# A two-layer decoder trunk: the down projection of 16 FFN slices as seven products per set, between gate and up chunks

## The chip, the cores and the metric

The kernel runs on one core of a Trainium2 chip. The metric is the device time in microseconds (us) of one execution. PE is TensorE, which multiplies matrices (PEld is its loading of the stationary operand); DVE is VectorE, ACT is ScalarE, POOL is GpSimd, SP issues most of the DMAs.

## The reference

Two layers on 512 tokens of width 1024. Layer 0 mixes tokens by sliding-window attention, layer 1 by a chunked spatial gating unit; each layer then has a SwiGLU FFN. Every mixer and every FFN stands between two RMS norms and adds to the residual:

```python
def swiglu(h, w_gate_up, w_down):
    gu = h @ w_gate_up                                        # 1024 -> 2 x 2816
    return (jax.nn.silu(gu[..., :D_FF]) * gu[..., D_FF:]) @ w_down   # 2816 -> 1024

for i in range(DEPTH):
    m = swa_sink_attention(rmsnorm(x, ...), ...) if i % 2 == 0 else chunked_sgu(rmsnorm(x, ...), ...)
    x = x + rmsnorm(m, norm_mix_post[i])
    x = x + rmsnorm(swiglu(rmsnorm(x, norm_ffn_pre[i]), w_gate_up[i], w_down[i]), norm_ffn_post[i])
```

Everything is float32. The 2816 hidden units of an FFN are 22 slices of 128.

## The kernel before, in words

**Numbers in two parts.** PE multiplies a float32 number as a high part in a rounded format and a low part, the rest. So every product is three matmuls (`mm3`): high by high, high by low, low by high. What PE reads has to be split first: ACT copies the high part (`wh`, L257), DVE subtracts it from the raw number for the low part (`wl`, L253).

**Weights as one stream.** All weights lie in device memory in the order of their use, in chunks of 8 blocks of 128 x 128 (512 KB). `fetch` has SP load a chunk into one of `NRAW` = 2 raw tiles; `split` makes it into a `wh` and a `wl` tile of a ring of `NW` = 17 tiles of 4 KB per partition, in which row vectors also lie for a while. `blk` gives PE a block and counts how often a chunk is still needed; a chunk that nobody needs is given back.

**Order of the work.** The order of the instructions of PE, DVE and ACT is written out by a planner in the kernel itself: it keeps a clock for PE (`now`) and one for each helper, and runs small generators (`Side`) when they are due. `split_idle` decides when the next chunk is split: never before the previous one has issued its low part; at once when its slack has sunk to a margin of the stage (`PLAN`, first number: 2.0 in stage 2, 8.0 in 3, 10.0 in 6, 6.0 in 7); otherwise only when the helpers are idle and no generator marked as a chain is due soon. The slack is the number of chunks ahead times `pace` less a constant:

```python
slack = max(now[0], hold[0]) + (c - cur[0] - 1) * pace[0] - max(now[0], busy["v"], busy["a"]) - 2.4
```

**The FFN** (`ffn`). PE computes gate and up of one slice (48 matmuls of 512 columns: 8 depth blocks, two outputs, three passes), ACT takes silu from PSUM (L614), DVE multiplies by up (L620), ACT and DVE split the result (L624, L627). The first three slices run in two halves of the tokens. After 11 slices their down projection follows: for each column half all four token tiles of 128 tokens at once (`tok_proj`), ACT copies the results to `m` (L678). After the other 11 slices comes the second half of the down projection, first column half for all tokens, then the second column half token by token; DVE adds the result to `m` (L689), and `Tok` runs the token's norm and residual (squares on ACT, the gain on DVE or POOL L509/L503, the reciprocal root on DVE, L522) while PE goes on with the next token. For the next layer the tokens are scaled, transposed by PE (L459) and split (L472, L476). In the last FFN the last token's second column half is computed in two parts of 256 columns (L711), and the rows are stored.

**Attention and the gating layer** use the same ring. Tiles of the tag `rt` (three of 2 x 512) hold pairs of high and low parts there; `p` tiles (two of 4 x 512) hold scores, later gating inputs.

Of the kernel before, what the change touches and what calls it, by code (L numbers as in the profile page):

```python
# [6 lines left out]
F32 = mybir.dt.float32  # L7
# [13 lines left out]
HJ = NJ // 2  # L21
# [4 lines left out]
NW = 17  # L26
# [5 lines left out]
NRAW = 2  # L32
# [16 lines left out]

V0 = 0  # L50
# [5 lines left out]
SV0 = GU0 + 3 * NJ * KT  # L56
# [5 lines left out]
NBLK = GU1 + 3 * NJ * KT  # L62

def uses(i):

    if i < Q0 or WO0 <= i < GU0 or SO0 <= i < GU1:
        return 4
    if SV0 <= i < SO0:  # L70
        return 4 if i < SU0 or SV1 <= i < SU1 else 2 if i < SV1 else 1
    if i < WO0:
        return 1
    b = i - GU0 if i < SV0 else i - GU1
    f, b = divmod(b, 3 * HJ * KT)
    if b >= 2 * HJ * KT:
        return 4
    return 2 if f == 0 and b < 3 * 2 * KT else 1
# [3 lines left out]
def trunk_kernel(ctx, tc, x_t, xt, w, cols, rows, ws_t, consts, out):  # L82
# [136 lines left out]
    left = [0] * NCH  # L219
    for i in range(NBLK):  # L220
        left[i // CB] += uses(i)

    def fetch(free=0.0, most=NBLK):
        while len(raws) < min(NCH, len(chunks) + NRAW, most):
            c = len(raws)
            if c == NLATE:
                load_x()
            if c == NLATE + 1:
                nc.sync.dma_start(c_msk[:, 0:256], consts[:, 1024:1280])
                nc.sync.dma_start(c_msk[:, 256:384], consts[:, 1408:1536])  # L230
                nc.sync.dma_start(cs[:], consts[:, 0:1024])
                busy["d"] += 2.5
            raw = rawp.tile([P, CB * P], F32, tag="raw", name=nm("raw"))
            nc.sync.dma_start(raw[:], w[c])
            busy["d"] = max(busy["d"], now[0], free) + 1.46
            raws[c] = (raw, busy["d"] + DLAT)

    def split():
        c = len(chunks)
        fetch()  # L240
        raw, ready = raws[c]
# [68 lines left out]
    def drop(n=1):  # L310
        used[0] -= n

# [296 lines left out]
    def ffn(base, nx_in, g1o, nx_out):  # L609
# [30 lines left out]

        h = hsrc(nx_in)

        def gu(g, b0, j, hf):
            grab("acc")
            grab("acc")
            ps = (acc(), acc())
            for k in range(KT):
                rh, rl = h(k, hf)
                for u in range(2):
                    wh, wl = blk(b0 + (j * KT + k) * 2 + u)  # L650
                    mm3(ps[u][:, hf], wh, wl, rh, rl, k == 0, k == KT - 1)
                tick()
            evac_gu(g, j, *ps, hf)

        m = None
        for f in range(2):
            stage[0] = (2 if base == GU0 else 6) + f
            b0 = base + f * (HJ * KT * 3)
            ga = [gp.tile([P, 8, S], F32R, tag="ga", name=nm("ga")) for _ in range(2)]
            gb = [gp.tile([P, 3, S], F32R, tag="gb", name=nm("gb")) for _ in range(2)]  # L660
            g = [[ga[i][:, k] if k < 8 else gb[i][:, k - 8] for k in range(HJ)] for i in range(2)] + [{}]
            j0 = 0
            if f == 0:
                pace[0] = 2.5
                for hf in halves:
                    for j in range(3):
                        gu(g, b0, j, hf)
                j0 = 3
            pace[0] = 5.1
            for j in range(j0, HJ):  # L670
                gu(g, b0, j, full)
            d0 = b0 + HJ * KT * 2
            l = gsrc(g)
            if f == 0:
                m = new_m()
                for c in range(2):
                    def evac0(t, ps):
                        nc.scalar.activation(m[t][c][:], ps[:], AF.Copy)  # L678
                        A(S, now[0] + 0.2)
                    tok_proj(d0 + c * HJ * 4, HJ, l, evac0)  # L680
                continue
# [10 lines left out]
            tok_proj(d0, HJ, l, lambda t, ps: add(t, 0, ps), False)  # L692
            hold[0] = now[0] + NB * HJ * 0.65
            for t in range(NB if nx_out is not None else NB - 1):
                grab("acc")
                ps = acc()
                for k in range(HJ):
                    tok_mm(ps, l, t, k, d0 + HJ * 4 + 4 * k, k == 0, k == HJ - 1)
                add(t, 1, ps)
            if nx_out is None:  # L700
                t = NB - 1
                until(lambda: toks[0].done)
                for i, hf in enumerate(halves):
                    grab("acc")
                    ps = acc()[:, 0:256]
                    for k in range(HJ):
                        lh, ll = l(k, slice(t * P, (t + 1) * P))
                        wh, wl = blk(d0 + HJ * 4 + 4 * k, 4 if i else 0, 4)
                        mm3(ps, lh, ll, wh[:, hf], wl[:, hf], k == 0, k == HJ - 1)
# [3 lines left out]
            drop()  # L713


    def attention(nx_in, g1o, nx_out):
# [263 lines left out]
        hold[0] = now[0] + NB * 8 * 0.65 + 10  # L980
        for t in range(NB):
            tok = Tok(t, m[t], g1, nx_out)
            for c in range(2):
# [7 lines left out]
        drop(2)  # L991


    def sgu(nx_in, g1o, nx_out):
# [157 lines left out]
        drop()  # L1152
# [73 lines left out]
def _layout(inputs):  # L1226
# [30 lines left out]
    def ffn(i):  # L1257
        gu = blocks(a["ffn_w_gate_up"][i]).reshape(KT, 2, NJ, P, P)
        dn = blocks(a["ffn_w_down"][i])
        for h in range(2):  # L1260
            js = slice(h * HJ, (h + 1) * HJ)
            seq.append(gu[:, :, js].transpose(2, 0, 1, 3, 4).reshape(-1, P, P))
            for c in range(2):
                seq.append(flat(dn[js][:, 4 * c:4 * c + 4]))
# [12 lines left out]
    assert w.shape[0] == NBLK  # L1277
    w = np.ascontiguousarray(w.reshape(NBLK // CB, CB, P, P).transpose(0, 2, 1, 3).reshape(NBLK // CB, P, CB * P))

# [40 lines left out]
```

## Time and profile before

| | |
|---|---|
| median of 3 runs | 1066.5 us (1066.02 to 1067.13) |
| the profiled execution | 1067.36 us, its span 1065.6 us |
| mean granted clock | 0.994 |
| PE, DVE, ACT busy | 1046.0, 524.8, 438.4 us |
| matmuls, weight splits | 5237 recorded, 176 |
| read from device memory | 102.13 MB |

The profile is of one execution. Busy time of PE counts matmuls that overlap in its pipeline, so it says little about how well PE is fed; the chain of work and the list of waits say more. The last pieces of the down projections end at about 365, 549, 874 and 1059 us.

### The profile page before, as it was taken

To read this page: it belongs to the slowest core of one execution; us is meant where nothing else is said; L and a number is where in the kernel's file an instruction comes from. 1 tells how busy PE (TensorE), PEld (TensorE's weight loads), DVE (VectorE), ACT (ScalarE), POOL (GpSimd) and SP (SyncE) were. 2 spreads that over 40 slices of the span, in tenths; PEclk is the share of its full clock that TensorE was granted. 3 is DMA by queue.
4 is the path that set the end of the run, shared out by engine and by line. 5 is a ranking of instruction groups with operands and counts; after the bars stand their busy time and mean duration, and the time that the engine had idled before them with its cause. 6 is when DMAs were issued, how large, how long until landed. Compare 5 with 4: busy or idle time off the path is not lost.

```text
span 1065.6 us, 13311 instructions
## 1 busy us (share of the span) xinstructions
PE 1046.0 (98%) x5237; PEld 869.6 (82%) x5237; DVE 524.8 (49%) x1074; ACT 438.4 (41%) x775; POOL 24.2 (2%) x22
## 2 busy tenths in 40 slices
PE   7998998999999999999999999999999999999997
PEld 6875666988888888888889888899888888888886
DVE  6699679743332233332474867584333223333335
ACT  4799676632322223222255444573223222232210
POOL 2000002000000000000000000100000000000000
PEclk9999999999999999999999999999999999999999
DMA  8322101433233322223133233034223332222302
GB/s 292 125 93 80 60 21 60 131 127 99 99 99 99 99 99 95 94 92 135 59 119 100 79 125 106 28 120 151 90 97 98 99 99 99 99 99 98 101 1 80
DMA packets 29839, 105.10 MB, mean 99 GB/s; under 512 B 3344, under 2 KB 3872, under 8 KB 29776
## 3 DMA queue, kind: packets, MB, share of 16 engines
q1 hardware_dynamic: 29088, 103.10, 29.1%
q8 instruction: 41, 0.67, 0.3%
q10 hardware_dynamic: 576, 0.92, 0.2%
q0 software_dynamic: 112, 0.23, 0.2%
q14 instruction: 22, 0.18, 0.0%
HBM read 102.13 MB, written 2.10 MB: 98 GB/s over the span
## 4 chain that ended last, share of the span: by engine, by line
PE 88%; DVE 7%; ACT 2%; DMA 1%; issue 1%; POOL 0%; DVEq 0%; ACTq 0%; POOLq 0%
PE acc L204 86%; DVE wl L253 1%; DVE p L828 1%; ACT rt L746 1%; PE aux L459 1%; DVE p L859 1%; DMA raw<-w 1%; PE acc L888 1%; DMA c_cols<-cols 1%; PE aux L896 0%; DVE rt L740 0%; ACT wh L257 0%; ACT p L850 0%; DVE hl L1168 0%; PE aux L457 0%
## 5 line engine op out<-in xcount | busy, mean ns | idle before, releaser
L253 DVE TENSOR_TENSOR wl<-raw,wh 128x1024 fp32r<-128x1024 f32 x174 | 214.5, 1234 | 413.0 <-PE acc L204 340.4
L204 PE MATMUL acc<-hh,wh 128*128 128x512 f32 (+1 forms) x960 | 352.1, 367 | 0.0
L204 PE MATMUL acc<-hl,wh 128*128 128x512 f32 (+1 forms) x960 | 349.8, 364 | 0.0
L204 PE MATMUL acc<-hh,wl 128*128 128x512 f32 (+1 forms) x960 | 349.7, 364 | 0.0
L257 ACT ACTIVATE wh<-raw 128x1024 fp32r<-128x1024 f32 x176 | 185.8, 1058 | 220.4 <-PE acc L204 184.6
L204 PE MATMUL acc<-wh,ga 128*128 128x512 f32 (+1 forms) x736 | 236.2, 392 | 2.7 <-DVE ga L915 2.7
L204 PEld LDWEIGHTS acc<-hh,wh 128*128 128x128 f32 x960 | 181.0, 188 | 29.1 <-issue 0.2
L204 PEld LDWEIGHTS acc<-hh,wl 128*128 128x128 f32 x960 | 180.9, 188 | 28.9
L204 PEld LDWEIGHTS acc<-hl,wh 128*128 128x128 f32 x960 | 181.0, 189 | 28.8 <-issue 0.2
L204 PEld LDWEIGHTS acc<-wh,ga 128*128 128x128 f32 x736 | 138.3, 189 | 35.1 <-issue 4.9
L204 PE MATMUL acc<-wl,ga 128*128 128x512 f32 (+1 forms) x368 | 142.3, 387 | 0.0
L614 ACT ACTIVATE t<-acc 128x512 f32<-128x512 f32 (+1 forms) x50 | 27.3, 545 | 146.5 <-PE acc L204 146.5
L204 PEld LDWEIGHTS acc<-wl,ga 128*128 128x128 f32 x368 | 69.8, 190 | 12.8
L204 PE MATMUL acc<-wh,gb 128*128 128x512 f32 (+1 forms) x198 | 61.9, 383 | 0.0
L624 ACT ACTIVATE ga<-t 128x512 fp32r<-128x512 f32 (+1 forms) x38 | 21.5, 565 | 53.5 <-DVE t L620 53.4
L204 PEld LDWEIGHTS acc<-wh,gb 128*128 128x128 f32 x198 | 36.9, 188 | 7.2
L503 POOL TENSOR_TENSOR m<-m,row 128x512 f32<-128x512 f32 x12 | 17.2, 1433 | 1020.6 <-ACT acc L381 1020.6
L204 PE MATMUL acc<-wh,hh 128*128 128x512 f32 (+1 forms) x96 | 34.4, 368 | 4.4 <-ACT wh L257 4.4
L204 PE MATMUL acc<-wl,gb 128*128 128x512 f32 (+1 forms) x99 | 37.9, 383 | 0.0
L381 ACT ACTIVATE acc<-m 128x512 f32<-128x512 f32 x30 | 18.0, 598 | 46.5 <-DVE m L689 42.1
L204 PE MATMUL acc<-wh,hl 128*128 128x512 f32 (+1 forms) x96 | 34.3, 367 | 0.7 <-DVE hl L1168 0.7
L627 DVE TENSOR_TENSOR ga<-t,ga 128x512 fp32r<-128x512 f32 (+1 forms) x38 | 23.1, 607 | 21.1 <-ACT ga L624 21.1
(124 smaller groups left out, 830.4 us busy)
## 6 DMA issues: line engine op xcount, KB each, us to landing
raw<-w SPq DMA_DIRECT2D x176, 512.0 KB, 3.5
row<-rows SPq DMA_DIRECT2D x8, 512.0 KB, 4.5
xg<-xt SPq DMA_DIRECT2D x4, 512.0 KB, 7.3
x<-x_t SPq DMA_DIRECT2D x4, 512.0 KB, 7.3
out<-x SPq DMA_DIRECT2D x4, 256.0 KB, 2.1
out<-x ACTq DMA_DIRECT2D x3, 256.0 KB, 2.1
cs<-consts SPq DMA_DIRECT2D x1, 512.0 KB, 7.2
t<-ws_t SPq DMA_DIRECT2D x2, 256.0 KB, 4.3
```

What stands on the lines that cost most here:

```text
L204: nc.tensor.matmul(ps, a, b, start=start, stop=stop)
L253: nc.vector.tensor_tensor(wl[:], raw[:], wh[:].bitcast(F32), ALU.subtract)
L257: nc.scalar.activation(wh[:], raw[:], AF.Copy)
L381: nc.scalar.activation(junk, src, AF.Square, accum_out=s[:, c:c + 1])
L459: nc.tensor.transpose(dst, self.src[t][k // 4][:, (k % 4) * P:(k % 4 + 1) * P], ident)
L503: nc.gpsimd.tensor_tensor(self.m[c][:], self.m[c][:], self.g1[:, cols2[c]], ALU.mult)
L614: nc.scalar.activation(t1[:, hf], pg[:, hf], AF.Silu)
L624: nc.scalar.activation(g[0][jj][:, hf], t1[:, hf], AF.Copy)
L627: nc.vector.tensor_tensor(g[1][jj][:, hf], t1[:, hf], g[0][jj][:, hf].bitcast(F32), ALU.subtract)
L746: nc.scalar.activation(ro[o:o + 32, hf], t1[q * 32:q * 32 + 32, hf], AF.Identity, bias=b[q * 32:q * 32 + 32])
L828: nc.vector.tensor_tensor_reduce(pt[:, 2 * g2 + g, i, 0:nk], sc[i][:, g * 256:g * 256 + nk], mask[:, 256 - nk:256], 0.125, sink_bc[:, pr * ...
L859: nc.vector.tensor_scalar(p(j), p(j), sm[:, j:j + 1], None, ALU.mult)
```

## The change

Of the 22 slices of an FFN the first 16 go through the down projection in two sets of eight (`SETS`). In a set the hidden units are taken in quads of four slices. Tokens are cut into two halves of 256, hidden units into two parities (even and odd slices of the quad), output columns into two halves of 512. The 2 x 2 by 2 x 2 block product is formed by seven block products instead of eight (`PRODUCTS`: which two blocks of the activations and which two of the weights are added or subtracted first; `TARGETS`: where each result is added or subtracted).

- The weights of a product with two blocks are loaded as two raw tiles, added on DVE and then split; `NRAW` is 4, `NW` is 15, `fetch` counts raw tiles.
- Slices 0 to 15 are kept unsplit after silu and product (`evac_raw`). A chain generator (`operands`) adds two blocks on DVE where needed and splits the sum into one of three `rt` tiles, up to three ahead of PE.
- `ITEMS` is the order of PE's work: items of a product and a quad (12 matmuls), alternating with items of half a slice of gate and up (24 matmuls). The first set's products run between slices 8 to 15, the second's between slices 16 to 21.
- `settle` adds a product's two PSUM banks to the rows of `m` (the first set's first contributions are copied by ACT).
- The last six slices run as before per token tile, but tokens 0 and 1 together, then token 2, then token 3, each with both column halves.
- The row tile of the gain is counted as free only after its tokens have used it (`drop_after`), in attention and gating too; gating gives its `rt` tiles back.
- The host lays the down weights out by quad, parity and column half.

```diff
-NW = 17
+NW = 15
...
-NRAW = 2
+NRAW = 4
+SETS = (8, 8)
+AJ = sum(SETS)
+BJ = NJ - AJ
+NQ = AJ // 4
...
+PRODUCTS = (
+    (((0, 0), (1, 1), 1), ((0, 0), (1, 1), 1)),
+    (((1, 0), (0, 0), -1), ((0, 0), (0, 1), 1)),
+    (((1, 1), None, 0), ((1, 0), (0, 0), -1)),
+    (((0, 1), (1, 1), -1), ((1, 0), (1, 1), 1)),
+    (((0, 0), None, 0), ((0, 1), (1, 1), -1)),
+    (((0, 0), (0, 1), 1), ((1, 1), None, 0)),
+    (((1, 0), (1, 1), 1), ((0, 0), None, 0)),
+)
+TARGETS = (
+    (("=", 0, 0), ("=", 1, 1)),
+    (("+", 1, 1),),
+    (("=", 1, 0), ("+", 0, 0)),
+    (("+", 0, 0),),
+    (("=", 0, 1), ("+", 1, 1)),
+    (("+", 0, 1), ("-", 0, 0)),
+    (("+", 1, 0), ("-", 1, 1)),
+)
...
+        ps = [("p", (n, p), q) for p in range(len(PRODUCTS)) for q in range(q0, q0 + SETS[n] // 4)]
+        gs = [("g", j, half) for j in range(j0, j1) for half in range(2)]
+        np_, ng = len(ps), len(gs)
+        while ps or gs:
+            out.append(gs.pop(0) if gs and len(gs) * np_ >= len(ps) * ng else ps.pop(0))
...
-        while len(raws) < min(NCH, len(chunks) + NRAW, most):
+        while len(raws) < min(NCH, most) and raw_used[0] + len(STREAM[len(raws)][0]) <= NRAW:
...
+            raw_used[0] -= 1
...
+        def high_low(f):
+            yield f
+            nc.scalar.activation(wh[:], raw[:], AF.Copy)
+            yield from low(A(CB * P, f))
+        if len(tiles) == 2:
+            op = ALU.add if STREAM[c][1] > 0 else ALU.subtract
+            nc.vector.tensor_tensor(raw[:], raw[:], tiles[1][:], op)
+            f = V(CB * P, ready)
+            raw_used[0] -= 1
+            fetch(f)
+            chunks[c] = [wh, wl, None, None, f]
+            chunks[c][2] = Side(high_low(f), f)
+            return
...
-        slack = max(now[0], hold[0]) + (c - cur[0] - 1) * pace[0] - max(now[0], busy["v"], busy["a"]) - 2.4
+        slack = max(now[0], hold[0]) + (c - cur[0] - 1) * pace[0] - max(now[0], busy["v"], busy["a"]) - (2.4 if len(STREAM[c][0]) == 1 else 3.7)
...
+    def drop_after(toks):
+        def side():
+            while any(len(t.half) < 2 for t in toks):
+                yield now[0] + 0.2
+            drop()
...
+        stage[0] = 2 if base == GU0 else 6
...
+        def operands():
+            for n, (p, q) in enumerate(todo):
+                while n >= spent[0] + len(ring):
+                    yield now[0] + 0.2
...
+                    yield from take("t")
+                    t = tmp()[:].rearrange("p (a t) -> p a t", a=2)
+                    nc.vector.tensor_tensor(t, src, view(y), ALU.add if sign > 0 else ALU.subtract)
+                    src = t
...
+                hi, lo = (r.rearrange("p (a t) -> p a t", a=2) for r in ring[n % len(ring)])
+                nc.scalar.activation(hi, src, AF.Copy)
+                f = A(S, f)
+                yield f
+                nc.vector.tensor_tensor(lo, src, hi.bitcast(F32), ALU.subtract)
+                made[p, q] = V(S, f), hi, lo
...
+        Side(operands(), now[0], True)
+        pace[0] = 4.0
...
+        def settle(p, ps):
+            for sign, th, c in TARGETS[p[1]]:
+                for i in range(2):
+                    d = m[2 * th + i][c][:]
+                    if sign == "=" and not p[0]:
+                        nc.scalar.activation(d, ps[i][:], AF.Copy)
                         A(S, now[0] + 0.2)
...
+                    else:
+                        nc.vector.tensor_tensor(d, d, ps[i][:], ALU.subtract if sign == "-" else ALU.add)
+                        V(S, now[0] + 0.2)
...
+                q0 = sum(SETS[:a[0]]) // 4
+                last = q0 + SETS[a[0]] // 4 - 1
+                if b == q0:
+                    banks = two()
+                until(lambda: (a, b) in made)
+                f, hi, lo = made[a, b]
+                wait(f)
+                for kp in range(2):
+                    for i in range(2):
+                        ts = slice(i * P, i * P + P)
+                        wh, wl = blk(at + 4 * kp, 4)
+                        mm3(banks[i][:], hi[:, kp, ts], lo[:, kp, ts], wh, wl,
+                            b == q0 and kp == 0, b == last and kp == 1)
+                        tick()
+                spent[0] += 1
+                if b == last:
+                    settle(a, banks)
+                    give("acc")
+                    give("acc")
+            at += CB
...
+        pace[0] = 5.1
+        stage[0] += 1
...
+            ends = [(0, 0), (0, 1), (1, 0), (1, 1)]
+            if nx_out is None:
+                ends.pop()
+            ends = [((0, 1), 0), ((0, 1), 1)] + [((2 + i,), c) for i, c in ends]
+            for n, (ts, c) in enumerate(ends):
+                if n == 2:
+                    hold[0] = now[0] + 4 * BJ * 0.65
+                for t in ts:
+                    grab("acc")
+                ps = [acc() for _ in ts]
+                for k in range(BJ):
+                    for t, q in zip(ts, ps):
+                        tok_mm(q, l, t, k, d0 + c * BJ * 4 + 4 * k, k == 0, k == BJ - 1)
+                for t, q in zip(ts, ps):
+                    add(t, c, q)
```

## Rows read from the trace of the kernel before

**Rows 1.** The clocks: the span in us from the first to the last instruction and the mean granted clock of TensorE.

```profile
core 0: 1065.6 us, clock 0.994
```

**Rows 2.** The page, part 1: busy time of each engine, its share of the span, its instructions.

```profile
PE 1046.0 (98%) x5237; PEld 869.6 (82%) x5237; DVE 524.8 (49%) x1074; ACT 438.4 (41%) x775; POOL 24.2 (2%) x22
```

**Rows 3.** The chain of work that ended last, in order of time, pieces merged: start, length in us, what it is. The two longest pieces.

```profile
205.46 336.82 PE acc L204 x1548
...
714.43 344.14 PE acc L204 x1617
```

**Rows 4.** The list of waits: who waited for whom, total us, times, longest. The first three from 205 to 1059 us, the last for PE alone from 175 us on.

```profile
DVE wl L253 <- PE acc L204: 340.4, 100, 4.6
ACT wh L257 <- PE acc L204: 184.6, 67, 4.4
...
ACT wh L257 <- DMA raw<-w: 28.0, 21, 4.1
...
PE acc L204 <- DVE ga L915: 2.7, 1, 2.7
```

**Rows 5.** The timeline of DVE, GpSimd and PE in two places of the attention stage: start, us, engine, line, operation, tiles, count, and in brackets the idle time before it and what ended it.

```profile
71.80 2.35 DVE L253 TENSOR_TENSOR wl<-raw,wh 128x1024 fp32r<-128x1024 f32 x2
...
171.19 1.62 POOL L503 TENSOR_TENSOR m<-m,row 128x512 f32<-128x512 f32 x1 [2.08 <-ACT acc L381]
171.59 2.29 DVE L253 TENSOR_TENSOR wl<-raw,wh 128x1024 fp32r<-128x1024 f32 x1
...
174.54 1.20 PE L204 MATMUL acc<-wh,ga 128*128 128x512 f32 x2 [2.67 <-DVE ga L915]
```

**Rows 6.** The timeline of PE: first and last of 28 consecutive matmuls of 512 columns in the second FFN, and first and last of 30 of 256 columns in the gating layer.

```profile
799.79 0.39 PE L204 MATMUL acc<-hl,wh 128*128 128x512 f32 x1
...
805.91 0.39 PE L204 MATMUL acc<-hl,wh 128*128 128x512 f32 x1
...
560.32 0.28 PE L204 MATMUL acc<-hh,wh 128*128 128x256 f32 x1
...
563.79 0.28 PE L204 MATMUL acc<-hh,wl 128*128 128x256 f32 x1
```

**Rows 7.** Groups by line from 205 to 1059 us, DVE and ACT: busy us, mean ns of one, then the idle time before them.

```profile
L253 DVE TENSOR_TENSOR wl<-raw,wh 128x1024 fp32r<-128x1024 f32 x148 | 181.8, 1229 | 411.9 <-PE acc L204 340.4 <-ACT wh L257 71.3
L620 DVE TENSOR_TENSOR t<-t,acc 128x512 f32<-128x512 f32 (+1 forms) x47 | 29.6, 629 | 0.0
L627 DVE TENSOR_TENSOR ga<-t,ga 128x512 fp32r<-128x512 f32 (+1 forms) x36 | 22.2, 618 | 21.1 <-ACT ga L624 21.1
L689 DVE TENSOR_TENSOR m<-acc,m 128x512 f32<-128x512 f32 x15 | 10.0, 688 | 24.3 <-PE acc L204 24.3
...
L257 ACT ACTIVATE wh<-raw 128x1024 fp32r<-128x1024 f32 x148 | 156.4, 1058 | 212.7 <-PE acc L204 184.6 <-DMA raw<-w 28.0
L614 ACT ACTIVATE t<-acc 128x512 f32<-128x512 f32 (+1 forms) x47 | 26.1, 556 | 145.8 <-PE acc L204 145.8
L624 ACT ACTIVATE ga<-t 128x512 fp32r<-128x512 f32 (+1 forms) x36 | 20.6, 573 | 53.5 <-DVE t L620 53.4
```

**Rows 8.** Stretches: from and to in us, length, then busy us and instructions of PE, PEld, DVE, ACT and POOL, the granted clock, the DMA share, GB/s.

```profile
15.00:20.00 5.00, 4.28 (x36) 4.08 (x35) 4.63 (x6) 2.29 (x5) 0.75 (x1) 1.00 1.01 390
25.00:30.00 5.00, 5.00 (x22) 3.79 (x21) 2.41 (x5) 0.77 (x2) 0.00 (x0) 1.00 0.28 98
120.00:125.00 5.00, 5.00 (x24) 3.04 (x22) 2.59 (x6) 1.59 (x4) 0.00 (x0) 1.00 0.89 313
165.00:170.00 5.00, 5.00 (x23) 2.64 (x23) 4.90 (x13) 3.96 (x10) 1.30 (x1) 1.00 0.26 74
170.00:175.00 5.00, 2.33 (x9) 1.65 (x9) 4.88 (x6) 2.44 (x7) 1.62 (x1) 0.96 0.11 39
175.00:180.00 5.00, 5.00 (x20) 4.07 (x20) 4.96 (x23) 1.67 (x3) 1.29 (x1) 0.70 0.29 99
205.00:317.00 112.00, 112.00 (x560) 95.53 (x559) 42.81 (x50) 37.67 (x50) 0.00 (x0) 1.00 0.33 106
```

**Rows 9.** What SP's queue waited for (total us, times, longest), and the weight loads among the DMA issues of the page (count, KB each, median us from issue to landing).

```profile
SPq L234 <- DVE wl L253: 823.7, 158, 30.8
...
raw<-w SPq DMA_DIRECT2D x176, 512.0 KB, 3.5
```

**Rows 10.** The timeline where the first FFN hands over to the gating layer: token 0's and token 1's last down halves (L689), the first transposes (L459), the first matmul of the next layer and the last low part of tokens 0 and 1 (L476).

```profile
525.32 0.69 DVE L689 TENSOR_TENSOR m<-acc,m 128x512 f32<-128x512 f32 x1 [2.81 <-PE acc L204]
528.69 1.41 DVE L522 SCALAR_TENSOR_TENSOR x<-m,rc,x 128x512 f32<-128x512 f32 x2
532.80 0.69 DVE L689 TENSOR_TENSOR m<-acc,m 128x512 f32<-128x512 f32 x1 [2.70 <-PE acc L204]
542.12 0.60 PE L459 MATMUL aux<-c_id,m 128*128 128x128 f32 x4
549.34 0.48 PE L204 MATMUL acc<-wh,hh 128*128 128x512 f32 x1
551.49 0.87 DVE L476 SCALAR_TENSOR_TENSOR hl<-aux,c_cols,hh 128x256 fp32r<-128x256 f32 x2
```

**Rows 11.** The end of the same chain as in rows 3: start, length in us, what it is.

```profile
1058.60 0.44 DVE m L711
...
1062.03 0.40 DVE x L567
```

More of the change, by code (lines that the diff above doesn't have):

```diff
@@ L20 @@
 NJ = FF // P
-HJ = NJ // 2
 EPS = 1e-6
@@ L61 @@
 GU1 = SO0 + 64
[L62 to L78, printed above, removed]
+NBLK = GU1 + FFB
 @with_exitstack
@@ L232, in fetch @@
                 busy["d"] += 2.5
[L233 to L236, printed above, removed]
+            tiles = []
+            for b in reversed(STREAM[c][0]):
+                raw = rawp.tile([P, CB * P], F32, tag="raw", name=nm("raw"))
+                nc.sync.dma_start(raw[:], w[b])
+                busy["d"] = max(busy["d"], now[0], free) + 1.46
+                tiles.insert(0, raw)
+            raw_used[0] += len(tiles)
+            raws[c] = (tiles, busy["d"] + DLAT)
     def split():
@@ L240, in split @@
         fetch()
-        raw, ready = raws[c]
+        tiles, ready = raws[c]
+        raw = tiles[0]
         assert used[0] + 2 <= NW
@@ L311, in drop @@
         used[0] -= n
+    def drop_after(toks):
[3 more added lines that the diff above has]
+            drop()
+        Side(side(), now[0])
     xs = [xp.tile([P, D], F32, tag=f"x{k}", name=f"x{k}") for k in range(NB)]
@@ L644, in gu, with two @@
+        h = hsrc(nx_in)
+        def gu(ps, b, js, hf):
+            for k in js:
+                rh, rl = h(k, hf)
+                for u in range(2):
+                    wh, wl = blk(b + 2 * k + u)
+                    mm3(ps[u][:, hf], wh, wl, rh, rl, k == 0, k == KT - 1)
+                tick()
+        def two():
             grab("acc")
             grab("acc")
[L646 to L678, printed above, removed]
-                        A(S, now[0] + 0.2)
-                    tok_proj(d0 + c * HJ * 4, HJ, l, evac0)
-                continue
+            return acc(), acc()
@@ new lines, in ffn, with quad @@
+        pa = [ptile() for _ in range(2)]
+        g8 = gp.tile([P, 8, S], F32, tag="ga", name=nm("ga"))
+        ga = gp.tile([P, 8, S], F32R, tag="ga", name=nm("ga"))
+        gb = [gp.tile([P, 3, S], F32R, tag="gb", name=nm("gb")) for _ in range(2)]
+        cells = [ga[:, k] for k in range(8)] + [gb[i][:, k] for i in range(2) for k in range(3)]
+        g = [cells[0:BJ], cells[BJ:2 * BJ], {}]
+        raw_ready = {}
+        def quad(q):
+            return pa[q] if q < 2 else g8[:, 4 * q - 8:4 * q - 4]
@@ new lines, in raw_g, with parity, pair_tile @@
+        def raw_g(j):
+            return quad(j // 4)[:, j % 4]
+        def parity(q, e):
+            return quad(q)[:].rearrange("p (a b) t -> p b a t", b=2)[:, e]
+        def pair_tile(dt=F32):
+            grab("rt")
+            return tp.tile([P, 2, S], dt, tag="rt", name=nm("rt"), bufs=3)
+        stage[0] = 2 if base == GU0 else 6
+        pace[0] = 2.5
+        for hf in halves:
+            for j in range(3):
+                ps = two()
+                gu(ps, base + j * 2 * KT, range(KT), hf)
+                evac_raw(raw_g(j), j, *ps, hf, raw_ready)
@@ new lines, in ffn @@
+        for kind, a, b in ITEMS:
+            if kind == "g":
+                if b == 0:
+                    gps = two()
+                gu(gps, at - b * CB, range(4 * b, 4 * b + 4), full)
+                if b and a < AJ:
+                    evac_raw(raw_g(a), a, *gps, full, raw_ready)
+                elif b:
+                    evac_gu(g, a - AJ, *gps, full)
+            else:
+                q0 = sum(SETS[:a[0]]) // 4
[11 more added lines that the diff above has]
+                            b == q0 and kp == 0, b == last and kp == 1)
+                        tick()
+                spent[0] += 1
+                if b == last:
+                    settle(a, banks)
+                    give("acc")
+                    give("acc")
+            at += CB
@@ L682, in ffn @@
+        for _ in range(3):
+            give("rt")
+        pace[0] = 5.1
+        stage[0] += 1
+        d0 = at
+        l = gsrc(g)
+        if 1:
             spare[0] = 0
@@ L1151, in sgu @@
             evac(t, 1, ps)
-        drop()
+        drop_after(toks)
+        for _ in range(NY):
+            give("rt")
     n0, n1, n2, n3 = (NextH(i) for i in range(4))
```

125 lines of the change are left out of this document (100 added, 25 removed).

## The prediction

> **What bounds the kernel now.** I read the mean clock first: one core, 1065.6 us from the first to the last instruction at 0.994 of the full clock [rows 1], so the granted clock explains nothing over the whole. The table of engines comes next: PE is busy 98% of the span, DVE 49%, ACT 41% [rows 2]. A busy PE can still hide waits, so the chain of work that ended last is the view that decides [rows 3]. The reader is to see two long unbroken pieces in it, 336.82 us from 205.46 and 344.14 us from 714.43, both of matmuls at line 204: the two FFNs are chains of matmuls and of nothing else. The list of waits says the same from the other side [rows 4]: after 205 us DVE waits 340.4 us and ACT 184.6 us for PE, and of PE's own waits from 175 us on there is one row, the end of a wait that began earlier. That one is 2.67 us long and over at 174.54; PE waited for a DVE instruction that stood behind a split of 2.29 us [rows 5].
>
> Inside an FFN every 512-column matmul follows the one before it at a fixed pitch. From 799.79 to 805.91 there are 27 steps, so 226.7 ns each; a 256-column one takes 29 steps from 560.32 to 563.79, so 119.7 ns [rows 6]. A matmul taken out of an FFN is therefore worth 0.2267 us as long as PE goes on waiting for nobody.
>
> **What the products remove.** Sixteen of 22 slices, four token tiles, two column halves, three passes (high by high, high by low, low by high): 384 matmuls per FFN in the old down projection. New: two sets, seven products, two quads, 12 matmuls (two slice pairs, two token tiles, three passes): 336. So 48 fewer per FFN, 96 in all, and 96 x 0.2267 = 21.8 us off the path. The last token's second column half is computed in two 256-column parts; it now takes 36 such matmuls where it took 66. Per column these are dearer by 2 x 119.7 - 226.7 = 12.7 ns a pair, and 15 pairs fewer give another 0.2 us. Sum: -22.0 us.
>
> The Trainium skill ("TensorE: Matmul & The Clock Gate", section "Back-to-back issue gap") gives about 216 ns for such a matmul; by that the 96 would be worth 20.7 us. The trace has 226.7, and I use that.
>
> **What the products add, and what covers it.** Durations are means after 205 us [rows 7]: split's low part on DVE 1.229 us, its high part on ACT 1.058, a 512-wide DVE subtract from SBUF 0.618, a product with a PSUM input 0.629, an add from PSUM into SBUF 0.688, a 512-wide ACT copy 0.573. No row shows the 1024-wide sum of two raw weight tiles; it has the shape and kind of the low part and I give it 1.229 too. Its bounds are 1.13 (what the second of two in a row adds) and 2.29, the longest low part, which met a GpSimd multiply [rows 5].
>
> Per quad the weights are now 7 combined tiles where there were 4: three more splits and five sums; the activations 7 splits and five sums where there were 4 splits; the results 24 PSUM operations per set, of which 8 of the first set are on ACT. By stretch:
> - First set, with slices 8 to 15: 14 product items of 12 matmuls and 16 gate/up items of 24, 552 x 0.2267 = 125.1 us of PE. DVE: 30 low parts 36.9, ten weight sums 12.3, 24 operand operations 14.8, 16 results 11.0, eight products 5.0, together 80.0 us or 64%.
> - Second set, with slices 16 to 21: 14 and 12 items, 456 x 0.2267 = 103.4 us of PE. DVE: 26 low parts 32.0, ten sums 12.3, 24 operand operations 14.8, 24 results 16.5, six products and six splits 7.5, together 83.1 us or 80%. ACT: 27.5 + 8.0 + 6.8 = 42.3 us.
> The stretch from 205 to 317 has DVE at 42.81 of 112 us, 38% [rows 8]; what is new fits under PE by total. It also fits by order. Weights are split one after another, a chunk begins when the one before it has issued its low part, and the operand chain polls as a chain side for as long as products are left, which holds every split back until it is urgent. In the first FFN (margin 2.0, pace 4.0) that is when the chunk to split is two ahead of the one in use: the slack is 4.0 - 2.4 or 4.0 - 3.7. From there PE has one product (2.72 us) and one gate/up item (5.44 us) to run, 8.16 us, twice the worst chain of sum, high and low (3.5 us); with four result adds (2.8 us) ahead of the low part it is 6.3 us. Where two products stand together the next chunk is a gate/up one, 2.3 us of chain for 5.44 us of cover. I take +1 us for waits in the four stretches, bounds 0 and +11 (a fifth of a microsecond for each of 56 product items). If the cover fails, PE waits at the head of the next item, and the result adds wait behind it in DVE's queue, as they need PE's end.
>
> Transfers: a quad loads 12 tiles of 512 KB where it loaded 4, 64 more in all. The second set moves 36 in 103.4 us, 183 GB/s, and the core has moved 390 GB/s [rows 8]. SP's queue waits 823.7 us for freed raw tiles, and a load lands 3.5 us after its issue [rows 9]: loads go out when a tile is freed, not when the link has room. Four tiles instead of two let the next pair be on its way while the present one is split. Cost nothing; the cover is the same 8.16 us.
>
> **Last six slices.** Tokens 0 and 1 go together, then 2, then 3. Six new weight chunks are first used at 2.72 us each (12 matmuls), where the old order took 5.44. A split costs 1.06 on ACT and 1.23 on DVE; nothing is late. The handover to the spatial gating layer is what I expect to lose. Now token 1's second half is added at 532.80, its transposes begin at 542.12, and the next layer's first matmul, at 549.34, comes 7.2 us after them [rows 10]; the last low part of token 1 ends at 552.36, and is used at about 549.34 + 7 x 0.68 = 554.1. So there are 1.7 us in hand. After the change tokens 0 and 1 end 4 x 18 x 0.2267 = 16.3 us ahead of that matmul, 1.3 earlier than now (2 x 33 x 0.2267 = 15.0). But both arrive at once, and the work of token 0 (add, gain, reciprocal root, 525.32 to 530.10 without 1 us of waits, some 4 us of DVE) stands in the same window. Net 2.7 us later against 1.7 in hand: +1 us, bounds 0 and +4 (the whole of token 0's work).
> At the end of the program the last chain from 1058.60 (add, square, root, scale, store) is untouched [rows 11]. Token 2's chain ends 8.4 us ahead of PE's end where it was 7.9: 0.
>
> **The narrower ring.** 15 tiles hold seven weight chunks instead of eight; the row tile is held until its tokens have used it. In attention DVE is full at its end (4.90, 4.88, 4.96 of 5 us from 165 to 180) and has room at 120 to 125 (2.59) [rows 8]. A split that can't be made early lands in the full part: +1.2 us each, for one or two. Against that, loads are two tiles further ahead, and DVE has room at 25 to 30 (2.41), so splits may leave the full part: -1.2 each. And the order around the wait of 2.67 us changes, which may go or grow. I take 0, bounds -4 (that wait and its clock, and one split) and +4.
> Here the clock belongs: after that wait the stretch from 175 to 180 ran at 0.70 [rows 8], so part of it at the lower of the two levels, 1.2 and 2.4 GHz, and a wait costs more than its length. The Trainium skill ("TensorE: Matmul & The Clock Gate", section "HAM oscillation — how this bites in real kernels") warns that an idle gap of PE returns the clock to half, and would make stalls of some microseconds between products dearer than they look. The trace agrees for this one gap; no row shows it in an FFN.
>
> **Sum.** The profiled execution took 1067.36 us, 0.9 above the median of 1066.5. 1067.4 - 22.0 + 1 + 1 + 0 = 1047.4; on the scale of the median 1046.5.
>
> **Rivals.**
> 1. DVE's queue is late now and then: each product item waits 0.2 us, 56 x 0.2 = 11 us more, 1057. For: 80% in the second set, with result adds bound to PE's end in the same queue; against: 8.16 us of cover for 6.3.
> 2. Attention and the handovers pay for the ring: +4 and +4 in place of 0 and +1, 1053.5. For: DVE full from 165 to 180; against: as much work leaves that window as enters it.
> 3. The deeper raw buffer lets attention go, and the FFNs hide all: -4, and neither of the two single microseconds, 1040.5. For: ACT waits 28.0 us for raw loads even after 205 us [rows 4]; against: PE was fed through most of attention.
> 4. Slower. In the second set the work of one product runs as one chain through DVE and ACT, with no overlap of neighbours: 12/14 of a gate/up split (2.29) = 1.96, the product's split with 5/7 of a sum 3.17, its operand 5/7 x 0.62 + 0.57 + 0.62 = 1.63, its results 24/14 x 0.688 = 1.18, and 0.9 for the new slice's own evacuation; 8.8 us against 7.38 of PE. 1.46 x 28 = 41 us; 1046.5 + 41 = 1087. The first set (8.93 us of PE) would just hold. It decides when the chain passes 7.38 + 22/28 = 8.2 us. For: each split waits for the one before it; against: a neighbour starts as soon as the low part is issued, and ACT and DVE can work on two chunks.
>
> **How the numbers follow.** Forecast 0.63, with its own range 1042 to 1051; rival 1 0.14, rival 2 0.09, rival 3 0.06, rival 4 0.08. The range for 8 in 10 takes in rivals 2 and 3 and rival 1 to its 11 us: 1040 to 1058; outside are rival 4 and the tails. A measurement of this kernel tells 0.2%, 2.1 us. Faster 0.89 (all but rival 4 and a piece of rival 1), same 0.02, slower 0.09.
>
> **What would show it.** Right: 96 fewer 512-wide matmuls' worth of PE, the pitch still 226.7 ns, chain pieces of PE alone through both sets, DVE near 64% and 80% there, the list of waits after 205 us without PE but for about a microsecond at the handover. Rival 1: PE waits for the low part or for the operand tile, tenths of a microsecond, many times. Rival 2: PE's first matmul of the first FFN later than now. Rival 4: PE's share in the second sets near 85%, the clock below 1. The forecast is wrong if PE's waits in the FFNs exceed 5 us.

## The result and the profile after

1059.07 us, median of 4 runs (1058.15 to 1060.11), against 1066.82 for the kernel before on the same chip; ratio 0.9928 [0.9911, 0.9945]. The change gains 7.75 us, 0.7%; the forecast was 20 us, and its range ended at 1058.

The span and the engines of the profiled execution, as in [rows 1, 2]:

```profile
core 0: 1057.5 us, clock 0.989
```

```profile
PE 1031.1 (97%) x5126; PEld 854.7 (81%) x5126; DVE 684.7 (65%) x1276; ACT 469.6 (44%) x817; POOL 23.8 (2%) x22
...
HBM read 135.69 MB, written 2.10 MB: 130 GB/s over the span
```

DVE has 160 us more work, the chip reads a third more weights, and the mean clock is lower. To see where the time went I cut both spans at the same four matmuls: the first gate matmul of FFN 0, the first matmul of the gating layer, the first gate matmul of FFN 1, and PE's last. The timeline of PE in the kernel before (two of the four; the others start at 549.34 [rows 10] and 1058.28):

```profile
183.09 0.28 PE L204 MATMUL acc<-hh,wh 128*128 128x256 f32 x1
...
695.25 0.28 PE L204 MATMUL acc<-hh,wh 128*128 128x256 f32 x1
```

and in the kernel after:

```profile
191.43 0.28 PE L272 MATMUL acc<-hh,wh 128*128 128x256 f32 x1
...
545.93 0.40 PE L272 MATMUL acc<-wh,hh 128*128 128x512 f32 x1
...
697.29 0.28 PE L272 MATMUL acc<-hh,wh 128*128 128x256 f32 x1
...
1049.30 0.28 PE L272 MATMUL acc<-wh,gb 128*128 128x256 f32 x1
```

The same cut for every run, in us (the differences of such rows). One of e1's four executions took 2211.52 us and is left out, so that e1's time below is the median of three.

| kernel | attention | FFN 0 | gating | FFN 1 | after PE's last | span |
|---|---|---|---|---|---|---|
| before | 183.09 | 366.25 | 145.91 | 363.03 | 7.3 | 1065.6 |
| after | 191.43 | 354.50 | 151.36 | 352.01 | 8.2 | 1057.5 |
| e1, two raw tiles in attention | 188.31 | 354.51 | 151.31 | 352.01 | 8.3 | 1054.4 |
| e2, before with 15 ring tiles | 188.38 | 365.91 | 146.12 | 363.01 | 7.3 | 1070.7 |
| e3, tokens 0 and 1 apart | 191.61 | 355.00 | 146.52 | 352.02 | 7.3 | 1052.4 |
| e4, e1 and e3 | 187.97 | 354.99 | 146.56 | 352.02 | 7.3 | 1048.8 |
| e5, e4 and the ring tiles back | 181.84 | 355.02 | 146.53 | 352.02 | 7.3 | 1042.7 |
| e6, ring 17, raw 2 | 183.31 | 389.98 | 152.66 | 382.72 | 8.3 | 1117.0 |
| e7, ring 16, raw 3 | 189.69 | 359.08 | 150.25 | 351.94 | 8.2 | 1059.2 |

The FFNs gained 11.75 and 11.02 us. Attention lost 8.34, the gating layer 5.45, the end 0.9. The two long pieces of the chain stand as before [rows 3], shorter and of matmuls only:

```profile
213.43 323.59 PE acc L272 x1491
...
717.62 327.67 PE acc L272 x1509
```

The list of waits of PE in the kernel after (who waited for whom, total us, times, longest):

```profile
PE acc L1108 <- ACT t L1120: 6.6, 3, 3.8
PE acc L272 <- ACT wh L344: 3.1, 1, 3.1
PE acc L272 <- DVE ga L1135: 2.9, 2, 2.6
PE acc L272 <- DVE hl L571: 2.7, 1, 2.7
```

These are the first four of eight rows. L1108, L1120 and L1135 are lines of attention, the `wh` wait is the program's start, and `hl` L571 is the low part of the gating layer's first input. No row of the list, shown or not, belongs to a product. Four stretches, the first and the second set of FFN 0 and of FFN 1 (from, to, length, then busy us of PE, PEld, DVE, ACT, POOL, granted clock, DMA share, GB/s), show DVE at 58% and 77% in FFN 0 and 62% and 73% in FFN 1 (64% and 80% were worked out), PE without a gap, and the full clock:

```profile
283.80:409.00 125.20, 125.20 (x554) 103.68 (x553) 72.18 (x84) 43.08 (x57) 0.00 (x0) 1.00 0.43 138
409.00:512.40 103.40, 103.40 (x458) 85.65 (x457) 79.74 (x95) 45.11 (x57) 0.00 (x0) 1.00 0.64 206
788.00:913.20 125.20, 125.20 (x555) 103.68 (x554) 77.05 (x88) 45.20 (x59) 0.00 (x0) 1.00 0.49 154
913.20:1016.60 103.40, 103.40 (x458) 85.65 (x457) 75.41 (x90) 42.72 (x54) 0.00 (x0) 1.00 0.52 169
```

So the question was not the products but two places that they don't touch: attention, in which the change alters the sizes of two buffers and the time at which the gain's row tile counts as free, and the joint between the FFN and the gating layer.

### The profile page after: what moved, and what is told of

The parts are those of the page before. It is cut to its first block, busy times and chain, and to the rows that moved or that the text cites. A ratio compares the mean times of both kernels' runs of the same rounds, so it can differ in the third digit from the quotient of the medians.

```text
span 1057.5 us, 13471 instructions
## 1 busy us (share of the span) xinstructions
PE 1031.1 (97%) x5126; PEld 854.7 (81%) x5126; DVE 684.7 (65%) x1276; ACT 469.6 (44%) x817; POOL 23.8 (2%) x22
## 4 chain that ended last, share of the span: by engine, by line
PE 92%; DVE 3%; ACT 2%; issue 1%; DMA 0%; POOL 0%; DVEq 0%; ACTq 0%; POOLq 0%
PE acc L272 89%; PE acc L1108 1%; PE aux L1116 1%; PE aux L554 1%; ACT p L1070 1%; DMA c_cols<-cols 0%; ACT rt L966 0%; DVE wl L325 0%; DVE x L617 0%; DVE hl L1393 0%; ACT wh L344 0%; PE aux L552 0%; ACT t L1120 0%; DVE m L1210 0%; DVE rc L471 0%
## 5 line engine op out<-in xcount | busy, mean ns | idle before, releaser
L325 DVE TENSOR_TENSOR wl<-raw,wh 128x1024 fp32r<-128x1024 f32 x198 | 241.9, 1230 | 151.1 <-PE acc L272 78.2
L272 PE MATMUL acc<-wh,rt 128*128 128x512 f32 x496 | 162.3, 389 | 0.0
L272 PE MATMUL acc<-wh,ga 128*128 128x512 f32 (+1 forms) x344 | 120.3, 399 | 3.6 <-DVE ga L1135 2.9
L272 PEld LDWEIGHTS acc<-wh,rt 128*128 128x128 f32 x496 | 93.1, 188 | 19.4
L272 PE MATMUL acc<-wl,rt 128*128 128x512 f32 x248 | 96.5, 389 | 0.0
L272 PEld LDWEIGHTS acc<-wh,ga 128*128 128x128 f32 x344 | 65.2, 191 | 21.1 <-DVE ga L1135 3.8
L853 DVE TENSOR_TENSOR m<-m,acc 128x512 f32<-128x512 f32 x80 | 51.8, 684 | 44.2 <-PE acc L272 33.0
L272 PE MATMUL acc<-wl,ga 128*128 128x512 f32 (+1 forms) x206 | 80.0, 388 | 0.0
L332 ACT ACTIVATE wh<-raw 128x1024 fp32r<-128x1024 f32 x40 | 42.3, 1059 | 71.0 <-DVE raw L337 71.0
L272 PEld LDWEIGHTS acc<-wl,rt 128*128 128x128 f32 x248 | 46.6, 188 | 9.6
L337 DVE TENSOR_TENSOR raw<-raw,raw 128x1024 f32<-128x1024 f32 x40 | 48.8, 1219 | 0.0
L272 PEld LDWEIGHTS acc<-wl,ga 128*128 128x128 f32 x206 | 39.3, 191 | 6.6
```

What stands on the lines that cost most here:

```text
L272: nc.tensor.matmul(ps, a, b, start=start, stop=stop)
L337: nc.vector.tensor_tensor(raw[:], raw[:], tiles[1][:], op)
L853: nc.vector.tensor_tensor(d, d, ps[i][:], ALU.subtract if sign == "-" else ALU.add)
```

## The experiments

Theory A: attention pays because splits of weights are made at other times, when the ring is smaller (a split has to wait) and when raw tiles are more (a split is made too early); the joint pays because tokens 0 and 1 arrive together. Rival B: attention pays because its instructions themselves run slower, with tiles and traffic in other places. e1 to e4 were compared with the kernel before at 1066.82 us, e5 to e7, on another chip, at 1065.31.

**e1: two raw tiles until FFN 0's weights are due.**

```diff
-... raw_used[0] + len(STREAM[len(raws)][0]) <= NRAW:
+... raw_used[0] + len(STREAM[len(raws)][0]) <= (2 if len(raws) < 20 else NRAW):
```

> The changed kernel, but as long as the first 20 weight chunks (those of attention) are being loaded, only two of the four raw tiles are used. The changed kernel starts the first gate/up matmul at 191.4 us, the kernel before at 183.1. Theory ring (15 instead of 17 tiles makes the splits late): the start stays at 191 +- 1 and the time at 1059. Theory raw (loads two tiles further ahead let splits be put between the steps of the rope and softmax chains, and PE waits for ACT there): the start falls to 183 to 186 and the time to 1051 to 1054.

Measured: 1056.21, ratio 0.9902 [0.9881, 0.9923]; attention 188.31 instead of 191.43, between what the two theories said: the raw tiles make a part of the loss, 3.1 us, and the ring is to make the rest. "Loads further ahead" cost where they were to help. The timeline of ACT and PE of the kernel after, around 98 us, shows how:

```profile
94.44 1.04 ACT L344 ACTIVATE wh<-raw 128x1024 fp32r<-128x1024 f32 x1
...
95.51 2.91 ACT L966 ACTIVATE rt<-rt,c_cols 32x512 f32<-32x512 f32 x4
...
98.86 0.58 ACT L1120 ACTIVATE t<-aux 128x512 f32<-128x512 f32 x1
...
99.49 1.97 PE L1108 MATMUL acc<-t,vt 128*64 128x512 f32 x2 [3.78 <-ACT t L1120]
```

With more raw tiles loaded, a chunk is split in an earlier free moment: the low part that runs at 87.79 in e1 runs at 80.79 here. Everything that was written out behind it got another order. Around 98 us a split and four rotations of 0.7 us each stand on ACT ahead of the copy of the transposed scores, and PE waits 3.78 us for it. In e1 two of these copies (93.73 and 94.78) run ahead of the split, and PE's longest wait there is 2.39 us. The stretch behind the wait ran at a granted clock of 0.50, which is 1.2 GHz, the lower level, throughout. In the kernel after:

```profile
99.49:105.00 5.51, 5.51 (x23) 3.38 (x24) 2.88 (x11) 1.88 (x4) 0.00 (x0) 0.50 0.13 54
```

and in e1, the wait and the stretch behind it:

```profile
100.80 0.65 PE L1116 MATMUL aux<-c_id,p 128*128 128x128 f32 x4 [2.39 <-ACT t L1120]
```

```profile
100.80:105.00 4.20, 4.20 (x21) 2.20 (x22) 4.13 (x12) 3.62 (x12) 0.00 (x0) 0.59 0.41 125
```

The new order has a third price. The matmuls `acc<-t,vt` hold only 64 columns of weights, and four of them take 1.08 us when they stand together, but two take 1.07 us when they stand alone. First e1, then the kernel after, where the second pair had to wait for its own copy:

```profile
91.78 1.08 PE L1108 MATMUL acc<-t,vt 128*64 128x512 f32 x4
```

```profile
91.69 1.07 PE L1108 MATMUL acc<-t,vt 128*64 128x512 f32 x2
93.05 1.07 PE L1108 MATMUL acc<-t,vt 128*64 128x512 f32 x2 [0.28 <-ACT t L1120]
```

Counted from the same matmul (88.51 us in e1, 88.17 in the kernel after) to the end of attention, the kernel after loses 3.5 us against e1. PE's waits sum to 10.8 us where they were 10.1; half of the time that PE worked at the lower clock is 6.1 us where it was 5.1; and the 56 matmuls `acc<-t,vt` take 4.2 us more than 14 x 1.08 us, the clock taken off, where it was 2.3. The sum, 0.7 + 1.0 + 1.9 = 3.6, agrees with the 3.5.

**e2: the kernel before with 15 ring tiles, and nothing else.**

```diff
-NW = 17
+NW = 15
```

> The kernel before with a ring of 15 tiles instead of 17, nothing else. Theory ring: the first gate/up matmul moves from 183.1 to 190 to 192 and the time rises by 7 to 10 us, to 1074 to 1077. Theory raw: the start moves by less than 2.5 us and the time stays within 1065 to 1070.

Measured: 1072.81, ratio 1.0062 [1.0045, 1.0079]; attention 188.38, 5.3 us later, everything behind it within 0.4. That too lies between the two theories, and at the place where e1 ends: the smaller ring is dear by itself, and makes what e1 left. The splits' low parts on DVE in the kernel before:

```profile
120.80 1.22 DVE L253 TENSOR_TENSOR wl<-raw,wh 128x1024 fp32r<-128x1024 f32 x1
151.53 1.23 DVE L253 TENSOR_TENSOR wl<-raw,wh 128x1024 fp32r<-128x1024 f32 x1
```

and in e2, with PE's first wait behind them:

```profile
134.69 1.22 DVE L253 TENSOR_TENSOR wl<-raw,wh 128x1024 fp32r<-128x1024 f32 x1
149.07 1.22 DVE L253 TENSOR_TENSOR wl<-raw,wh 128x1024 fp32r<-128x1024 f32 x1
...
148.72 1.07 PE L888 MATMUL acc<-t,vt 128*64 128x512 f32 x2 [2.58 <-ACT t L900]
```

Up to the low part at 118.07 (117.58 in e2) the order is the same. Then the split that DVE made at 120.80, where it had room [rows 8], finds the ring full: `cs`, `v4`, `bo` and six chunks are 15 tiles. It comes at 134.69, and all that was written out after it shifts; PE gets a new wait of 2.58 us, and three of 0.36 to 0.69 later. From the same matmul (89.03 us before, 88.58 in e2) to the end of attention PE waits 10.1 us where it waited 6.3, the lower clock takes 5.1 us where it took 3.4, and the pairs that stand alone 2.3 where it was 2.0: 3.8 + 1.7 + 0.3 = 5.8 us, against 5.7 by which PE falls back from there on. A split takes the usual 1.22 us in both, which speaks against rival B.

**e3: tokens 0 and 1 apart in the second column half.**

```diff
-ends = [((0, 1), 0), ((0, 1), 1)] + [((2 + i,), c) for i, c in ends]
+ends = [((0, 1), 0), ((0,), 1), ((1,), 1)] + [((2 + i,), c) for i, c in ends]
...
-if n == 2:
+if n == 3:
```

> The changed kernel, but in the last six slices token tile 0 ends its second column half before token tile 1 starts it (both still share the first half), in both FFNs. Theory handover (PE waits 2.7 us behind the first FFN because tokens 0 and 1 end together, and then runs at half clock): token 0 is done 4.1 us earlier, the wait for hl goes below 0.5 us, the gating layer from its first matmul to the second FFN's first gate/up matmul takes 146 to 148 us instead of 151.4, and the time falls by 3 to 5 us to 1054 to 1056. Rival (the wait comes from the order of splits and gains on DVE, whoever ends first): the wait stays at 2 to 3 us and the time within 1057 to 1060.

Measured: 1053.57, ratio 0.9877 [0.9859, 0.9895]; gating 146.52 instead of 151.36, the end 0.9 shorter, FFN 0 half a microsecond longer, attention as in the kernel after. This is what the theory of the handover said, and the time came out 0.4 us below its range. The wait for `hl` L571 is gone from PE's list. Around it the timeline of the kernel after reads (L901 the adds of down results, L617 the residual, L571 the low part for the gating layer):

```profile
528.20 1.37 DVE L901 TENSOR_TENSOR m<-acc,m 128x512 f32<-128x512 f32 x2 [5.30 <-PE acc L272]
...
534.74 1.41 DVE L617 SCALAR_TENSOR_TENSOR x<-m,rc,x 128x512 f32<-128x512 f32 x2
...
545.40 0.86 DVE L571 SCALAR_TENSOR_TENSOR hl<-aux,c_cols,hh 128x256 fp32r<-128x256 f32 x2
...
547.47 1.41 DVE L617 SCALAR_TENSOR_TENSOR x<-m,rc,x 128x512 f32<-128x512 f32 x2
...
550.54 0.87 DVE L571 SCALAR_TENSOR_TENSOR hl<-aux,c_cols,hh 128x256 fp32r<-128x256 f32 x2
...
551.07 0.50 PE L272 MATMUL acc<-wh,hl 128*128 128x512 f32 x1 [2.68 <-DVE hl L571]
551.93 0.64 PE L272 MATMUL acc<-wh,hh 128*128 128x512 f32 x1
...
555.35 0.47 PE L272 MATMUL acc<-wh,hl 128*128 128x512 f32 x1
```

Both tokens arrive at 528.20, token 1's residual ends at 536.15. The second pair of low parts stands in DVE's queue behind token 2's root and residual (547.47), the last add and a split, so PE waits 2.68 us. It is the second of four pairs, needed by the third of the eight depth blocks. Then eight matmuls from 551.93 to 555.35 take 427.5 ns each, the lower level's pitch, against 226.7 [rows 6]: 1.6 us more. In e3 token 0's residual runs at 528.35 instead of 532.19, token 1's at 532.99 instead of 534.74, and the first low parts at 540.63, 4.8 us earlier.

**e4: e1 and e3 together.**

> Both edits: two raw tiles during attention, and token tiles 0 and 1 apart. If the losses of attention and of the handover are independent, the gains of the two single edits add up within 1.5 us; by the theories raw and handover together the time is 1047 to 1050, by their rivals 1057 to 1060.

Measured: 1049.86, ratio 0.9844 [0.9827, 0.9860]. The two gains stand side by side: attention takes 187.97 as in e1, the gating layer 146.56 as in e3, and 9.2 us lie between the kernel after and e4 (2.9 by e1 alone, 5.5 by e3 alone, so 0.8 us more than their sum; 1.5 were allowed).

**e5: e4, with the ring's capacity in attention given back.** The two raw tiles that attention leaves idle take `v4` and `bo` out of the ring.

```diff
-        v4 = wp.tile([P, NB, 256], F32, tag="w", name=nm("vt"))
+        v4 = rawp.tile([P, NB, 256], F32, tag="raw", name=nm("vt"))
...
-        bo = row_tile(3)
+        bo = rawp.tile([P, D], F32, tag="raw", name=nm("row"))
+        nc.sync.dma_start(bo[:], rows[272 + 3 * D:272 + 4 * D].partition_broadcast(P))
```

> The kernel of run e4 (raw tiles held to two in the attention, tokens 0 and 1 apart), in which the attention gets back the ring tiles that it lost, at no memory: v4 and the bias row bo are put into the two raw tiles that the attention doesn't use. With 15 tiles and these two out of the ring, seven split chunks fit again beside cs, bo or g1, as before (17 tiles less three). Theory (all of the attention's loss is the order of the splits, which the ring's size sets; SBUF traffic of the wider FFN tiles, or the place of a tile, has nothing to do with it): the attention ends where it ended before, 183.1 us against 187.97 in run e4, with the splits of before at 120.8 and 151.5, the PE wait of 2.58 at 148.7 gone, and the time is 1049.9 less 4.9 = 1045.0 (1044 to 1046). Rival (one part of the loss is something else that came with the change, or the loads behind bo and v4 now wait): the attention stays at 186 to 188 and the time at 1048 to 1050.

Measured: 1044.65 us (1044.2 to 1045.0), ratio 0.9805 [0.979, 0.9819], 20.7 us faster than the kernel before and the best of all. Attention takes 181.84 us. The splits stand where they stood before:

```profile
119.53 1.22 DVE L325 TENSOR_TENSOR wl<-raw,wh 128x1024 fp32r<-128x1024 f32 x1
150.27 1.23 DVE L325 TENSOR_TENSOR wl<-raw,wh 128x1024 fp32r<-128x1024 f32 x1
```

and PE's waits there are those of the kernel before (0.91 us at 89.69, 2.40 at 100.68, 0.25 at 149.22, 2.67 at 173.28) and one of 0.72. Rival B falls: with the new tiles in place and the old order of splits, attention is as fast as before. e6 says the same with nothing moved: with 17 and 2 tiles the changed kernel's attention takes 183.31 us against 183.09, so the later release of the gain's row tile and the rest of the new program cost it no more than that.

**e6 and e7: what the raw tiles bought.** The kernel after with 17 ring and 2 raw tiles, and with 16 and 3.

```diff
-NW = 15
-NRAW = 4
+NW = 17
+NRAW = 2
```

> The change with the memory of before: 17 ring tiles and 2 raw tiles for the whole kernel. It prices the cover that the trade bought. Theory (the products need the raw tiles: a product chunk has two loads of 3.6 us, then an add of 1.2, a copy of 1.0 and a subtraction of 1.2 before both tiles are free, so some 10.6 us pass for one product with its gate/up half against 8.16 us of matmuls; 40 of the 56 products have two loads): attention 183, as before; waits PE <- wl or wh in both FFNs, 1 to 2.4 us at each of 40 products, so 1059.1 - 8.3 + 40 to 96 = 1091 to 1147. Rival (16 DMA queues at 130 GB/s have room, the ring's seven chunks hold enough, and two raw tiles would do): the FFNs stay at 354.5 and 352, time 1051.

> The change with 16 ring tiles and 3 raw tiles. Theory: in the FFNs three tiles let the load of the next chunk run while a product's pair is added and split, so most of what run e6 loses is back, but not all: waits of 0 to 0.5 us at 40 products, so 0 to 20 over the change's 1059.1; the attention has six chunks as with 15 (16 less three is 13), so it gains nothing from the ring tile and at most the 3.1 us of the raw tiles. Time 1056 to 1079. Rival (the loss in the attention is per ring tile, half of run e2's 5.3 comes back): attention 188.8 or less, and the FFNs unchanged: 1053 to 1056.

e6 measured 1112.38, ratio 1.044 [1.0423, 1.0458]. In its profiled execution, the longest of five (1118.8), attention is back at 183.31, and the FFNs lose 35.5 and 30.7 us. The chain that the forecast's cover hid now stands open (DVE's add of two raw tiles L337, ACT's copy L332, DVE's low part L325, and PE behind each):

```profile
436.62 1.23 DVE L337 TENSOR_TENSOR raw<-raw,raw 128x1024 f32<-128x1024 f32 x1 [2.57 <-DMA raw<-w]
...
437.88 1.06 ACT L332 ACTIVATE wh<-raw 128x1024 fp32r<-128x1024 f32 x1 [4.55 <-DVE raw L337]
438.97 1.23 DVE L325 TENSOR_TENSOR wl<-raw,wh 128x1024 fp32r<-128x1024 f32 x1 [1.12 <-ACT wh L332]
...
438.99 0.50 PE L272 MATMUL acc<-wh,rt 128*128 128x512 f32 x1 [0.63 <-ACT wh L332]
...
440.25 0.50 PE L272 MATMUL acc<-wl,rt 128*128 128x512 f32 x1 [0.76 <-DVE wl L325]
```

PE's waits for these two lines sum to 38.8 us in 45 pieces, none over 3.2:

```profile
PE acc L272 <- ACT wh L332: 22.9, 19, 3.2
PE acc L272 <- DVE wl L325: 15.9, 26, 0.8
```

With them the clock fell as well: PE worked some 26 us of the two FFNs at the lower level, which takes 13. Waits and clock make 52 of the 66 us; the other 14 were not taken apart. e7 measured 1063.08, ratio 0.9975 [0.9963, 0.9988], within its theory: three raw tiles leave four waits for the low part, 2.9 us in sum, all in FFN 0, which takes 4.6 us longer than in the kernel after; and 16 ring tiles hold no more chunks beside three others than 15 do (six). Attention takes 189.69, not the 188.8 of the rival. Of the three ways to cut the same memory, 15 and 4 was the best, and still not free.

## Why the prediction was wrong, step by step

- **"-22.0 us" for the matmuls: right.** FFN 1 is 11.02 us shorter, 48 x 0.2267 + 0.2 = 11.1. FFN 0's 11.75 is 0.9 more than its 48 matmuls, which is counted with the joint below.
- **"+1 us for waits in the four stretches": right, 0.** Rivals 1 and 4 did not come: a neighbour chunk starts while one is under way. In the kernel after the next chunk's copy on ACT begins at 443.17 us while the low part before it runs on DVE from 442.74 to 443.97. The sum of two raw tiles, 1.219 us on the mean of 40, was as estimated (1.229). DVE was a little less busy than the 64% and 80% worked out (58% and 77%, 62% and 73%).
- **"Cost nothing" for transfers: right, and e6 shows the cover.** With two raw tiles instead of four the two FFNs take some 66 us longer for the same transfers (in e6's profiled execution).
- **The narrower ring, "I take 0, bounds -4 and +4": the step that failed.** Measured +8.34. The ring gives +5.3 by itself (e2) and the raw tiles +3.1 (e1 against the kernel after). Two things were wrong in the step. "Loads are two tiles further ahead ... -1.2 each" had the wrong sign: a split that can be made earlier is one more instruction ahead of what PE waits for. And the price of a shifted split was counted as its own 1.2 us of DVE, whereas it sets the order of everything written out behind it: a new wait of PE of 2.6 us, one of 2.4 grown to 3.8, the clock after them, and matmuls of 64 columns pulled apart. From 89 us to attention's end PE's waits went from 6.3 to 10.8 us, what the lower clock takes from 3.4 to 6.1, and what the pairs alone take from 2.0 to 4.2: 4.5 + 2.7 + 2.2 = 9.4, against 9.2 by which PE falls back from there on (8.3, and 0.9 that it was ahead at 89 us).
- **The handover, "+1 us, bounds 0 and +4": right in kind, too small.** FFN 0 and gating together gained 6.3 us where the matmuls give 10.9, so it cost 4.6: the wait of 2.68, 1.6 us at the lower clock behind it, and 0.3 not assigned. That 2.7 us were forecast for the delay and a wait of 2.68 came is luck. Against the gating layer's first matmul the first low parts came 5.2 us later (545.40 to 545.93, before 543.64 to 549.34), and PE ran into the second of four pairs, whereas the 1.7 us in hand were read at the last. That the work of token 2, the last add and a split would stand in the same queue ahead of the low parts was left out.
- **"Token 2's chain ... : 0" at the end: +0.9.** The 8.4 and 7.9 us are right for token 2's last add (1041.23; before, 1050.69), not for the end of its chain, which lay 2.9 us ahead of PE's end in the kernel before (1055.70 against 1058.56). In the kernel after token 2's residual (1048.75 to 1050.16) stood ahead of the last token's adds, which PE's end at 1049.58 had released. In e3 the first part's add runs at 1043.31 and only the second part comes after PE's end.

Rival 2 (0.09) is the one that came, at 12.9 us instead of 8, and in attention not by its reason, DVE full from 165 to 180: the matmuls at 151.06 us in the kernel before already run 7.0 us later (158.04) in the kernel after. Put the measured sizes in for the two steps and the end, and take off the microsecond for the products: 1046.5 - 1 + 8.3 + 3.6 + 0.9 = 1058.3, against 1059.07.

The clock rule that I cited (the Trainium skill, "TensorE: Matmul & The Clock Gate", section "HAM oscillation — how this bites in real kernels": an idle gap of PE returns the clock to half) agrees with the two largest losses: 0.50 behind the wait of 3.78, 427.5 ns a matmul behind the wait of 2.68 (the last section has waits that it doesn't fit). I had it beside the forecast and put the clock into the lower bound alone, as something that may go, and not into the upper.

## What to carry to other kernels

A buffer traded from one stage to another has to be costed in every stage that uses it, and in a kernel whose order is planned the price isn't the work that moves but the new order behind it (waits, the clock after them, matmuls that no longer stand together); run the old kernel with the new buffer size alone before arguing. Where buffers of one stage lie idle in another (the raw tiles in attention), lend them out: that was worth 4 to 6 us here (4 by the ratios of e4 and e5, 6 in the attention of their profiled executions, of which 3 are clock), and cost no memory. At a joint between layers, end the first token as early as can be, not two at once.

## What was not expected of the hardware

- The same wait is followed by different clocks. PE waits 2.41 us at 101.36 in the kernel before and 2.40 us at 100.68 in e5. In both, the 5 us ahead of 100 us had the full clock. The stretches behind, first in the kernel before:

```profile
100.00:105.00 5.00, 3.65 (x22) 1.74 (x23) 4.95 (x11) 4.94 (x15) 0.00 (x0) 0.79 0.32 105
105.00:110.00 5.00, 5.00 (x30) 3.43 (x28) 3.18 (x13) 1.87 (x4) 0.00 (x0) 0.87 0.00 0
```

then in e5:

```profile
100.00:105.00 5.00, 3.62 (x26) 2.08 (x26) 4.90 (x14) 4.98 (x16) 0.00 (x0) 1.00 0.29 95
105.00:110.00 5.00, 4.97 (x29) 3.31 (x30) 4.86 (x22) 2.32 (x9) 0.00 (x0) 1.00 0.03 11
```

  The clock was given back for some 1.7 us (0.21 x 5 + 0.13 x 5). e5 was also 0.65 us ahead at 89 us and has the new wait of 0.72; in all its attention is 1.25 us shorter than that of the kernel before. The joint behind FFN 0 shows the same: in the kernel after the wait of 2.68 us was followed by 0.66, in e7 the same wait of 2.67 us, ended at 553.90, by the full clock. First the kernel after, then e7:

```profile
552.00:557.00 5.00, 5.00 (x17) 3.97 (x16) 4.91 (x8) 1.78 (x3) 0.00 (x0) 0.66 0.81 256
```

```profile
555.00:560.00 5.00, 4.80 (x22) 3.60 (x21) 4.97 (x10) 2.88 (x4) 0.00 (x0) 1.00 0.82 270
```

  What decides isn't visible in these rows, so a forecast of a wait is good only to what the clock may add.
- Two short waits can be followed by the lower clock as one long wait is, and mostly aren't. In e6 PE waits 1.01 and 0.76 us, ended at 358.10 and 359.36, and again 0.95 and 0.77 us, ended at 428.78 and 430.04; of fifteen such pairs two were followed by the lower clock. The stretches behind these two pairs:

```profile
360.00:365.00 5.00, 5.00 (x17) 3.92 (x16) 2.52 (x3) 1.59 (x2) 0.00 (x0) 0.66 0.62 209
430.00:435.00 5.00, 4.96 (x21) 3.98 (x22) 2.50 (x3) 1.69 (x2) 0.00 (x0) 1.00 0.54 158
```
